# Chunked scans joined into long ones, a modulation product moved from the output projection into the router, and unread products in layer two's router

## The chip, the cores and the metric

The kernel runs on one core of one Trainium2 chip, as a single launch. The metric is device time in microseconds (us), the median of the runs. The profile comes from one further execution that was recorded instruction by instruction. TensorE (PE in the profile), VectorE (DVE), ScalarE (ACT) and GpSimd (POOL) run beside each other; SyncE (SP) only issues transfers, as do GpSimd's queue entries marked DMA.

## The reference, cut to what matters

Two layers over 256 context tokens and 512 latent tokens, 1024 wide. The last layer needs only the latents' output.

```python
for l in range(DEPTH):                                  # DEPTH = 2
    mod   = silu(c)     @ w_ada[l] + b_ada[l]           # six shifts, scales and gates of 1024
    mod_c = silu(c_ctx) @ w_ada[l] + b_ada[l]           # the same for the context
    ...
    u = modulated_rmsnorm(x, ...) @ w_in[l]             # one combined projection
    # mLSTM, 4 heads, chunkwise: for each direction
    bc = jnp.cumsum(to_chunks(log_f), axis=-1)          # running sums that restart at every chunk
    m_t = jnp.maximum(inter, jnp.max(dlog, axis=-1))    # a running maximum of i - b inside the chunk
    h = h * rsqrt(mean(h * h) + EPS) * g_hnorm
    # convolution of width 31 + layernorm, and a 2-D Fourier mix, beside it
    x = x + gt1 * (mix_x @ w_out[l])                    # output projection
    # expert choice: every expert takes its top tokens
    aff = softmax(xn @ w_router); gate, idx = top_k(aff.T, 2 * n // 16)
    hid = silu(xs @ w_gate) * (xs @ w_up)               # 16 experts, xs the chosen rows
    x = x + gt2 * scatter(hid @ w_down * gate)
```

## The kernel before, in words

**Projections.** `w_in` and then `w_out` are read in blocks of 128 output columns. Each block's weights are split into a rounded part (ScalarE copy, L424) and the rest (VectorE subtraction, L425), two buffers deep: `next_w` asks for the split of the next block when a block begins, so that a split has one block's time, about 11 us in layer one, to be ready. The products are L490. `w_out` has eight blocks; VectorE adds each to the residual stream (L1234), ScalarE squares it (L1249).

**Work beside the products.** TensorE's order is the order in which the program issues. A generator that has something to do for TensorE is wrapped in a `Fill`: after each product step it gets credit in microseconds and issues as long as the credit lasts; `run_us(t)` issues about t us of it at once, `drain()` all that is left. On the other engines a scheduler sets the order when the kernel is built, each engine runs its list strictly in that order, and an instruction that waits holds all behind it.

**The chain.** `chain()` is the mLSTM of a layer, issued beside `w_in`. It takes the gates (128 rows: two directions by heads, 768 tokens in 6 chunks of 128), makes the running sums (12 scans of 64x128, L648 and L649) and running maxima (12 more, L655 and L657), state scans over the chunks (L669 to L672), and three exponentials of 128x768 on ScalarE: `WS` (L689), `FL` (L691) and `WI` (L694). Then `to_tokens` transposes the keys head by head (TensorE L626) into two banks that ScalarE copies out (L627). After the heads come the Fourier part (L885 on, copied out at L928), the convolution's layernorm (L950 is its first product; it needs the convolution, 62 VectorE operations at L1027), and the scaling of the heads' outputs (L878) ahead of their transposes.

**Layer two's modulation.** Its `w_ada`, 48 tiles of 0.5 MB, is needed late and is taken during layer one. Round 0 is `ada1()`: 16 loads of 0.5 MB issued by GpSimd (L284) and products on TensorE (L286, eight groups of 16 matmuls in the trace) beside layer one's `w_out`, then a small sum (L295). Rounds 1 and 2 are `ada1_rest()`: 32 loads (L1136) that VectorE multiplies and adds up (L1139 for the first of a run of eight, L1141 for the other seven), and `ada1_sums()` on TensorE (L1150, L1158).

**The router.** Logits are gathered during `w_out` and transposed (L1284); a softmax on VectorE and ScalarE gives the affinities, which TensorE transposes (L1311); VectorE finds the top tokens in rounds (L1318 to L1321) while TensorE transposes all tokens (L1335), copied out by ScalarE (L1336); the indices are transposed (L1357), and GpSimd gathers the rows (L1425, layer one) or TensorE selects them by products with one-hot matrices (L1433, L1448, layer two). The first expert's rows are transposed at L1451 in layer one.

**The experts.** SP loads weights in tiles of 1 MB (L1203) into a ring; `wide()` computes the products (L1505, L1515).

```python
fills.append(ada1f)          # round 0: beside layer one's w_out, at a rate
...
if not last:
    ada1f.run_us(ADA_XTK)    # what is left of it, after L1335
...
if not last:
    ada1f.drain()            # after L1357
```

## Time and profile before

| | us |
|---|---|
| median of three runs (lowest, highest) | 1813.42 (1810.08, 1815.36) |
| the profiled execution's own time | 1820.03 |
| its span in the trace | 1818.1 |
| TensorE busy | 1708.9 (94%) |
| VectorE busy | 655.8 (36%) |
| ScalarE busy | 445.1 (24%) |
| GpSimd busy | 124.2 (7%) |

The span runs from the first recorded instruction to the last; the profiled execution's own time is 1.9 us more. Times of day in the rows below are us from the span's start. [...]

### The profile page before, as it was taken

The numbers are of one execution on the slowest core, as the hardware profiler recorded it, in microseconds if no ns is written. First come the engines' busy times: TensorE is split into PE (matmuls) and PEld (weight loads), VectorE is DVE, ScalarE is ACT, GpSimd is POOL, SyncE is SP. The second block draws the span as 40 slices with busy tenths as digits, with TensorE's granted clock in tenths as the row PEclk, the third lists the DMA queues.
The fourth block names the chain that finished last, engine by engine and source line by source line (L and its number), as shares of the span: only waits on it lengthen the run. The fifth ranks groups of instructions, "written<-read, shape, count | busy, mean of one in ns | idle before, by whom it ended". The sixth has DMA issues, their size and how long they took to land. (4 is left out here: it accounts for less than half of the span.)

```text
span 1818.1 us, 27372 instructions
## 1 busy us (share of the span) xinstructions
PE 1708.9 (94%) x11544; PEld 944.9 (52%) x11544; DVE 655.8 (36%) x1420; ACT 445.1 (24%) x864; POOL 124.2 (7%) x183
## 2 busy tenths in 40 slices
PE   6989998997999999999899989989989999999997
PEld 3678986776333333333233467877644444344434
DVE  4623889754101001000013676965230222112213
ACT  4532453513101101011010553355221000010002
POOL 1011111210101101100100000020000000000000
PEclk8999999998899999999999999999989999999997
DMA  9456335944999999999995112243669999999993
GB/s 384 167 203 209 100 99 184 360 175 163 395 420 401 402 421 403 402 415 408 400 396 214 36 55 79 81 120 132 240 249 420 420 420 420 421 421 420 420 421 156
DMA packets 94523, 529.58 MB, mean 291 GB/s; under 512 B 10176, under 2 KB 13248, under 8 KB 45504
## 3 DMA queue, kind: packets, MB, share of 16 engines
q1 hardware_dynamic: 75776, 459.66, 62.9%
q0 software_dynamic: 18624, 68.17, 11.4%
q8 instruction: 91, 1.49, 0.3%
q14 instruction: 32, 0.26, 0.0%
HBM read 513.10 MB, written 14.68 MB: 290 GB/s over the span
## 5 line engine op out<-in xcount | busy, mean ns | idle before, releaser
L490 PE MATMUL PS<-RA,RB 128*128 128x512 f32 (+1 forms) x2352 | 517.5, 367 | 11.4 <-DVE RB L425 6.1
L490 PEld LDWEIGHTS PS<-RA,RB 128*128 128x128 f32 x2352 | 378.7, 193 | 87.0 <-issue 16.0
L1505 PE MATMUL PS<-A 128*32 128x512 f32 (+1 forms) x2264 | 410.0, 595 | 4.4 <-DMA A<-w_e_up 3.9
L1505 PE MATMUL PS<-WP,A 128*32 128x512 f32 (+1 forms) x2152 | 351.6, 597 | 4.0 <-DMA WP<-w_e_up 4.0
L1505 PEld LDWEIGHTS PS<-A 128*32 128x32 f32 (+1 forms) x2264 | 123.9, 122 | 236.4 <-issue 220.2
L1505 PEld LDWEIGHTS PS<-WP,A 128*32 128x32 f32 (+1 forms) x2152 | 102.0, 117 | 200.6 <-issue 189.4
L1515 PE MATMUL PS<-WP,A 128*32 128x512 f32 x816 | 112.3, 594 | 0.0
L1027 DVE SCALAR_TENSOR_TENSOR A<-A 128x783 f32<-128x783 f32 (+1 forms) x120 | 103.5, 888 | 0.1
L1456 ACT ACTIVATE A<-PS,A 128x128 f32<-128x128 f32 x80 | 35.9, 457 | 250.8 <-DVE A L1458 250.1
L1515 PE MATMUL PS<-A 128*32 128x512 f32 x656 | 95.0, 606 | 0.0
L424 ACT ACTIVATE RB<-A 128x1024 fp32r<-128x1024 f32 x60 | 63.3, 1058 | 128.4 <-PE PS L490 118.6
L1558 ACT ACTIVATE A<-PS 128x512 f32<-128x512 f32 x40 | 22.3, 595 | 294.0 <-PE PS L1557 294.0
L1604 DVE TENSOR_SCALAR A<-PS,A 128x512 f32<-128x512 f32 x6 | 4.5, 751 | 243.9 <-PE PS L1505 243.9
L1578 DVE SCALAR_TENSOR_TENSOR RB<-PS,A,RB 128x512 fp32r<-128x512 f32 x18 | 13.5, 750 | 205.7 <-ACT RB L1577 204.8
L1571 DVE SCALAR_TENSOR_TENSOR A<-PS,A 128x512 f32<-128x512 f32 x80 | 56.4, 746 | 86.2 <-PE PS L1570 85.6
L1458 DVE TENSOR_SCALAR A<-PS,A 128x128 f32<-128x128 f32 x80 | 32.6, 410 | 145.0 <-PE PS L1451 89.5
L425 DVE TENSOR_TENSOR RB<-A,RB 128x1024 fp32r<-128x1024 f32 x60 | 73.2, 1223 | 20.1 <-ACT RB L424 17.6
L1448 PEld LDWEIGHTS PS<-A 128*128 128x128 f32 x512 | 59.5, 196 | 7.2 <-DVE A L1549 4.9
L1448 PE MATMUL PS<-A 128*128 128x128 f32 x512 | 61.2, 281 | 0.4 <-DVE A L1435 0.4
L1549 DVE TENSOR_TENSOR A<-PS,A 128x512 f32<-128x512 f32 x32 | 22.1, 692 | 109.3 <-PE PS L1505 109.3
L1515 PEld LDWEIGHTS PS<-WP,A 128*32 128x32 f32 x816 | 27.9, 110 | 54.6 <-issue 54.6
L1570 PE MATMUL PS<-RB 128*128 128x512 f32 x160 | 46.4, 416 | 5.4 <-ACT A L1456 4.3
(343 smaller groups left out, 1576.5 us busy)
## 6 DMA issues: line engine op xcount, KB each, us to landing
A<-w_e_gate SPq DMA_DIRECT2D x73, 1024.0 KB, 17.3
A<-w_e_down SPq DMA_DIRECT2D x71, 1024.0 KB, 19.8
A<-w_e_up SPq DMA_DIRECT2D x65, 1024.0 KB, 15.8
WP<-w_e_up SPq DMA_DIRECT2D x63, 1024.0 KB, 15.5
WP<-w_e_gate SPq DMA_DIRECT2D x55, 1024.0 KB, 18.3
WP<-w_e_down SPq DMA_DIRECT2D x55, 1024.0 KB, 17.2
A<-w_ada POOLq DMA_DIRECT2D x80, 512.0 KB, 5.8
A<-w_in SPq DMA_DIRECT2D x44, 512.0 KB, 3.6
```

The source lines that it names most:

```text
L424: whi.append(act.activation(h, raw[i], AF.Copy))
L425: wlo.append(dve.tensor_tensor(lo, raw[i], h.bitcast(F32), OP.subtract))
L490: pe.matmul(banks[s][:, :LEN[s]], w[:, k], xin[:, j, k, OFF[s]:OFF[s] + LEN[s]], start=k == k0 and i == 0, stop=k == k1 and i == 2)
L1027: dve.scalar_tensor_tensor(o, i, wcol, o, op0=OP.mult, op1=OP.add)
L1448: pe.matmul(b[:, j], XT[2 + c][:, db * 128:db * 128 + 128], onehots[i][:, c], start=c == 0, stop=c == 3)
L1456: act.activation(dst[:, db], b[:, j], AF.Identity, bias=sh_, scale=sc_)
L1458: dve.tensor_scalar(dst[:, db], b[:, j], sc_, sh_, op0=OP.mult, op1=OP.add)
L1505: pe.matmul(B(o + hf)[c:c + wd, :], lhs(k, e)[:, c % 64:c % 64 + wd], w[e][:, a, hf * 512:hf * 512 + 512], start=k == 0, stop=k == KB - 1, ...
L1515: pe.matmul(B(o + 2)[32 * g:32 * g + 32, :], lhsc(k, e), w[e][:, a, hf * 512:hf * 512 + 512], start=k == 0, stop=k == KB - 1, tile_positio ...
L1558: act.activation(dst, b, AF.Copy)
L1570: pe.matmul(b, YS[:, j, db * 128:db * 128 + 128], PM if pm is None else pm, start=j == 0, stop=j == 1)
L1571: dve.scalar_tensor_tensor(X[LAT][:, db], b, MOD[l][:, LAT, 40 + db:41 + db], X[LAT][:, db], op0=OP.mult, op1=OP.add)
```

## The change

1. The 24 short scans of a layer become four scans of 64x768, two for the sums and two for the maxima. Two vectors of 768 that GpSimd writes (`RS`, ones with a zero at each chunk's start, and `RM`, zeros with -1e30 there) make them restart at each chunk.
2. The exponentials of `WI` and `FL` are tied behind the copies of the first and the second head's transposes, where they stood ahead of all of them.
3. The scaling at L878 (24 of 128x128 in layer one, 16 in layer two) goes from VectorE to ScalarE.
4. Round 0 of layer two's modulation leaves `w_out`. Its 16 loads get buffers of their own (nine and six of the former two rings and one more), are issued by GpSimd when the seventh of the eight blocks is reached in the program, and its products stand in three places of layer one's router: 24 matmuls after L1284, 24 after L1335, 16 after L1357, there with the sums of rounds 1 and 2 (L1150, L1158), which also leave `w_out`.
5. In layer two's router, three products of `ones` by a 512-wide tile are issued after L1284 and five after L1335, into a bank that nobody reads.

```diff
@@ chain()
+                for t, x, y in ((RS, 1.0, 0.0), (RM, 0.0, -1e30)):
+                    pool.memset(t, x)
+                    pool.memset(t[0:64, 0:TT:128], y)
+                    pool.memset(t[64:128, 127:TT:128], y)
...
-                for c in range(6):
-                    x0, x1 = c * 128, c * 128 + 128
-                    dve.tensor_tensor_scan(b_[fw, x0:x1], ones[fw], LF[fw, x0:x1], 0.0, op0=OP.mult, op1=OP.add)
...
+                dve.tensor_tensor_scan(b_[fw], RS[fw], LF[fw], 0.0, op0=OP.mult, op1=OP.add)
+                dve.tensor_tensor_scan(b_[bw][:, ::-1], RS[bw][:, ::-1], LF[bw][:, ::-1], 0.0, op0=OP.mult, op1=OP.add)
...
+                dve.tensor_tensor_scan(M[fw], RM[fw], a_[fw], -1e30, op0=OP.add, op1=OP.max)
...
-                after(act.activation(FL, FL, AF.Exp, scale=-1.0), kev, NOSYNC)
...
-                after(act.activation(WI, WI, AF.Exp), kev, NOSYNC)
                 for h in range(H):
                     yield from to_tokens(kT[:, h], h, KT)
+                    if h == 0:
+                        after(act.activation(WI, WI, AF.Exp), [kev[-1], tok[-1]], NOSYNC)
+                    if h == 1:
+                        after(act.activation(FL, FL, AF.Exp, scale=-1.0), [tok[-1]], NOSYNC)
...
-                            dve.tensor_scalar(hh, hh, SS[:, c0 + c, h:h + 1], None, op0=OP.mult)
+                            act.activation(hh, hh, AF.Copy, scale=SS[:, c0 + c, h:h + 1])
@@ layer two's modulation
+                def ada1_loads():
+                    for i in range(2 * KB):
+                        w0.append(V((areg[6:] + areg[:6] + [w0_r])[i], 4, 256))
+                        pool.dma_start(w0[i], w_ada[1, 0, i // KB, i % KB].rearrange("p (g c) -> p g c", g=4))
                 def ada1():
-                    yield from ada_round(1, 0, Ring(areg[:6]), 5, pool, some=ADS[1])
+                    ps = B(5)
+                    for i, w in enumerate(w0):
+                        k, hf = i % KB, i // KB
+                        for g in range(4):
+                            pe.matmul(ps[32 * g:32 * g + 32, hf * 256:hf * 256 + 256], cs[:, k, :], w[:, g],
+                                      start=k == 0, stop=k == KB - 1, tile_position=(0, 32 * g))
+                        if i % 2:
+                            yield 0.95
...
+                    yield from sums
...
-                fills.append(ada1f)
@@ w_out
                 if db == KB - 2 and not last:
                     ada1v.drain()
-                    fills.append(Fill(ada1_sums(), 0.6))
+                    ada1_loads()
@@ router
+            if last:
+                keep_up(3)
+            if not last:
+                ada1f.run_us(ADA_XTK[0])
...
+            if last:
+                keep_up(5)
...
-                ada1f.run_us(ADA_XTK)
+                ada1f.run_us(ADA_XTK[1])
...
+            def keep_up(n):
+                for _ in range(n):
+                    pe.matmul(B(7), ones, iot, start=True, stop=True)
```

How the change moves instructions, at two places. The first is layer one's chain. On VectorE, before, from the last of the running sums to the first of the running maxima (scans are listed as SCALAR_TENSOR_TENSOR; L425 is a weight split):

```order
L648 SCALAR_TENSOR_TENSOR A<-A 64x128
L649 SCALAR_TENSOR_TENSOR A<-A 64x128
L668 COPY A<-A 64x6
L651 TENSOR_TENSOR A<-A 128x768
L668 COPY A<-A 64x6
L425 TENSOR_TENSOR RB<-A,RB 128x1024
L655 SCALAR_TENSOR_TENSOR A<-A 64x128
```

and after (L653 and L654 are the long sums, L657 and L658 the long maxima, L670 the first state scan, L424 the weight split that was L425):

```order
L654 SCALAR_TENSOR_TENSOR A<-A 64x768
L669 COPY A<-A 64x6
L655 TENSOR_TENSOR A<-A 128x768
L666 MEMSET A 128x6
L669 COPY A<-A 64x6
L657 SCALAR_TENSOR_TENSOR A<-A 64x768
L658 SCALAR_TENSOR_TENSOR A<-A 64x768
L668 COPY A<-A 64x6
L676 MEMSET A 64x1
L668 COPY A<-A 64x6
L670 SCALAR_TENSOR_TENSOR A<-A 64x5
L424 TENSOR_TENSOR RB<-A,RB 128x1024
```

The split, which stood between sums and maxima, stands behind both. On ScalarE at the same place, before, from the table load ahead of the exponentials to the first copies of the keys' transposes:

```order
L684 ACT_TABLE_LOAD
L684 ACTIVATE A<-A 128x6
L689 ACTIVATE A<-A 128x768
L691 ACTIVATE A<-A 128x768
L694 ACTIVATE A<-A 128x768
L627 ACTIVATE A<-PS 128x2x128
L627 ACTIVATE A<-PS 128x4x128
```

and after (L690 is the exponential of `WS`, L626 the copies that were L627, L697 and L699 the other two exponentials):

```order
L685 ACT_TABLE_LOAD
L685 ACTIVATE A<-A 128x6
L690 ACTIVATE A<-A 128x768
L626 ACTIVATE A<-PS 128x2x128
L626 ACTIVATE A<-PS 128x4x128
L697 ACTIVATE A<-A 128x768
L626 ACTIVATE A<-PS 128x2x128
L626 ACTIVATE A<-PS 128x4x128
L699 ACTIVATE A<-A 128x768
```

Two exponentials have gone behind the first two and the first four copies. The second place is layer one's router. On TensorE, before, from the last logits to the first expert's rows:

```order
L1211 MATMUL PS<-A 32x512 x4
L1215 MATMUL PS<-A 32x512 x4
L1284 MATMUL PS<-A,WP_3273 128x17 x6
L1311 MATMUL PS<-A,WP_3273 96x128 x2
L1335 MATMUL PS<-A 128x128 x48
L1357 MATMUL PS<-A,WP_3274 128x96 x2
L1451 MATMUL PS<-A,WP_3274 128x128 x8
```

and after (L1317 is the former L1284, L1348 the former L1311, L1372 the former L1335, L1396 the former L1357; L1138 and L1148 are round 0, L1182 and L1190 the sums that were L1150 and L1158). A row of the list counts a float32 product once, which the trace shows as two instructions:

```order
L1317 MATMUL PS<-A,WP_3157 128x17 x6
L1138 MATMUL PS<-A 32x256 x24
L1348 MATMUL PS<-A,WP_3157 96x128 x2
L1372 MATMUL PS<-A 128x128 x48
L1138 MATMUL PS<-A 32x256 x24
L1396 MATMUL PS<-A,WP_3158 128x96 x2
L1138 MATMUL PS<-A 32x256 x16
L1182 MATMUL PS<-A 32x256 x16
L1148 MATMUL PS<-A 128x8 x4
L1190 MATMUL PS<-A 128x8 x8
L1490 MATMUL PS<-A,WP_3158 128x128 x8
```

All of the moved products stand in these three gaps. On GpSimd, before, the last loads of the modulation ahead of the router (L284 round 0, L1136 rounds 1 and 2):

```order
L1136 DMA A<-w_ada 128x1024
L284 DMA A<-w_ada 128x1024 x2
L1136 DMA A<-w_ada 128x1024 x7
L1278 MEMSET WP_3273 128x192
L1399 MEMSET A 128x16
```

and after (L1130 the loads of round 0, L1168 those of rounds 1 and 2):

```order
L1130 DMA A<-w_ada 128x1024
L1168 DMA A<-w_ada 128x1024 x8
L1130 DMA A<-w_ada 128x1024 x2
L1168 DMA A<-w_ada 128x1024
L1130 DMA A<-w_ada 128x1024 x4
L1168 DMA A<-w_ada 128x1024 x21
L1130 DMA A<-w_ada 128x1024
L1168 DMA A<-w_ada 128x1024
L1130 DMA A<-w_ada 128x1024 x8
```

Seven of round 0's sixteen loads are issued early, and nine, which go into the buffers of rounds 1 and 2, at the end, behind the last of those.

## Rows read from the trace of the kernel before

**Rows 1.** The page, part 1: busy us, share of the span, instructions of TensorE

```profile
PE 1708.9 (94%) x11544; PEld 944.9 (52%) x11544; DVE 655.8 (36%) x1420; ACT 445.1 (24%) x864; POOL 124.2 (7%) x183
```

**Rows 2.** Timeline, 74 to 97 us: start, us, engine, line, operation, idle before

```profile
76.01 0.42 DVE L648 TENSOR_TENSOR_SCAN A<-A 64x128 f32<-64x128 f32 x1
...
82.48 1.23 DVE L425 TENSOR_TENSOR RB<-A,RB 128x1024 fp32r<-128x1024 f32 x1
...
86.70 1.19 ACT L985 ACTIVATE A<-PS 128x512 f32<-128x512 f32 x1 [8.55 <-PE PS L490]
...
93.07 0.95 DVE L693 TENSOR_TENSOR A<-A 128x768 f32<-128x768 f32 x1
...
94.67 0.83 ACT L694 ACTIVATE A<-A 128x768 f32<-128x768 f32 x1
95.41 0.85 ACT L627 ACTIVATE A<-PS 128x256 f32<-128x256 f32 x2
...
95.82 0.69 PE L626 MATMUL PS<-A 128*128 128x128 f32 x2 [4.47 <-ACT A L627]
```

**Rows 3.** Busy by stretch, with TensorE's clock and the DMA share, around 98 us

```profile
96.00:102.00 6.00, 6.00 (x23) 5.23 (x24) 0.00 (x0) 1.56 (x4) 0.34 (x1) 0.53 1.00 390
```

**Rows 4.** Group of a short scan on VectorE: total busy us, mean ns

```profile
L669 DVE TENSOR_TENSOR_SCAN A<-A 64x5 f32<-64x5 f32 x1 | 0.2, 160 | 0.0
```

**Rows 5.** Timeline at the convolution's end, VectorE and TensorE

```profile
305.89 2.64 DVE L878 TENSOR_SCALAR A<-A 128x128 f32<-128x128 f32 x13
...
306.04 2.08 PE L950 MATMUL PS<-A 128*128 128x512 f32 x2 [5.55 <-DVE A L1027]
```

**Rows 6.** Timeline on ScalarE, Fourier part before the convolution's end

```profile
288.58 0.60 ACT L928 ACTIVATE A<-PS 128x512 f32<-128x512 f32 x1 [5.54 <-PE PS L926]
```

**Rows 7.** Groups on TensorE in layer one's output projection, 337 to 430 us

```profile
L286 PE MATMUL PS<-A 128*32 128x256 f32 x128 | 9.3, 413 | 0.0
...
L1150 PE MATMUL PS<-A 128*32 128x256 f32 x32 | 1.9, 382 | 0.0
L1158 PE MATMUL PS<-A 128*128 128x8 f32 x16 | 1.8, 251 | 0.0
...
L295 PE MATMUL PS<-A 128*128 128x8 f32 x8 | 1.0, 245 | 0.0
```

**Rows 8.** Groups on VectorE in the same stretch

```profile
L1141 DVE SCALAR_TENSOR_TENSOR A<-A 128x1024 f32<-128x1024 f32 x19 | 24.3, 1283 | 5.4 <-DMA A<-w_ada 5.2
```

**Rows 9.** Busy over the whole of the same projection

```profile
337.00:430.00 93.00, 92.87 (x643) 72.71 (x641) 49.06 (x65) 18.98 (x34) 13.99 (x27) 0.96 0.51 191
```

**Rows 10.** Timeline on TensorE in layer one's router

```profile
438.29 0.63 PE L1311 MATMUL PS<-A,WP 128*96 128x128 f32 x2 [3.30 <-DVE WP L1306]
...
449.87 0.58 PE L1357 MATMUL PS<-A,WP 96*128 96x96 f32 x2 [2.99 <-ACT WP L1354]
457.54 1.97 PE L1451 MATMUL PS<-A,WP 128*128 128x128 f32 x8 [7.09 <-DMA WP<-xrow,A]
```

**Rows 11.** Timeline of SP, the queue of the expert weights

```profile
460.22 3.01 SPq L1203 DMA_DIRECT2D WP<-w_e_gate  x2
```

**Rows 12.** Timeline on TensorE in layer two's chain

```profile
1088.05 7.64 PE L490 MATMUL PS<-RA,RB 128*128 128x512 f32 x25 [4.61 <-DVE RB L425]
...
1100.37 0.44 PE L626 MATMUL PS<-A 128*128 128x128 f32 x2 [3.31 <-ACT A L627]
```

**Rows 13.** Busy by stretch behind these two waits

```profile
1088.00:1092.00 4.00, 3.95 (x10) 3.18 (x11) 2.00 (x2) 0.00 (x0) 0.10 (x1) 0.57 0.64 165
1101.00:1106.00 5.00, 5.00 (x22) 3.99 (x21) 0.00 (x0) 1.59 (x4) 0.72 (x1) 0.66 0.40 131
```

**Rows 14.** Timeline on TensorE in layer two's router

```profile
1333.71 5.51 PE L1448 MATMUL PS<-A 128*128 128x128 f32 x32 [0.45 <-DVE A L1435]
...
1343.31 3.84 PE L1448 MATMUL PS<-A 128*128 128x128 f32 x32
```

**Rows 15.** Busy by stretch in layer one's experts

```profile
560.00:660.00 100.00, 100.00 (x920) 32.10 (x916) 8.19 (x15) 11.30 (x21) 10.04 (x8) 1.00 1.02 408
```

More of the change, by code (lines that the diff above doesn't have):

```diff
@@ L48 @@
 ADS = 2, 2
-ADA1_RATE, AREG, ADA_XTK = 0.3, 15, 1.2
+AREG, ADA_XTK = 15, (2.8, 2.8)
 NACC = 6
@@ L52 @@
 VLAG = 0.0, 2.5
-ADA1_LATE = 2.0
 WORDER = [[KB0 + i for i in range(4)] + p + [QB + i for i in range(4)] + [FB, FB + 1] + [OB + i for i in range(4)]
@@ L614, in body @@
             keep = {}
-            kev = []
+            kev, tok = [], []
             convq = []
@@ L626, in to_tokens @@
                         pe.transpose(p[:, c], src[:, (c0 + c) * 128:(c0 + c + 1) * 128], ident)
-                    act.activation(dst[:, c0:c0 + n, h, 0:128], p[:, 0:n], AF.Copy)
+                    tok[:] = [act.activation(dst[:, c0:c0 + n, h, 0:128], p[:, 0:n], AF.Copy)]
                     yield 0.22 * n
@@ L635, in chain @@
             def chain():
+                rs_r, RS = new(TT)
+                rm_r, RM = new(TT)
+                for t, x, y in ((RS, 1.0, 0.0), (RM, 0.0, -1e30)):
+                    pool.memset(t, x)
+                    pool.memset(t[0:64, 0:TT:128], y)
+                    pool.memset(t[64:128, 127:TT:128], y)
                 lf_r, LF = new(TT)
@@ L645, in chain @@
                 fw, bw = slice(0, 64), slice(64, 128)
-                for c in range(6):
-                    x0, x1 = c * 128, c * 128 + 128
-                    dve.tensor_tensor_scan(b_[fw, x0:x1], ones[fw], LF[fw, x0:x1], 0.0, op0=OP.mult, op1=OP.add)
-                    dve.tensor_tensor_scan(b_[bw, x0:x1][:, ::-1], ones[bw], LF[bw, x0:x1][:, ::-1], 0.0,
-                                           op0=OP.mult, op1=OP.add)
+                dve.tensor_tensor_scan(b_[fw], RS[fw], LF[fw], 0.0, op0=OP.mult, op1=OP.add)
+                dve.tensor_tensor_scan(b_[bw][:, ::-1], RS[bw][:, ::-1], LF[bw][:, ::-1], 0.0, op0=OP.mult, op1=OP.add)
                 dve.tensor_tensor(a_, G, b_, OP.subtract)
                 M = LF
-                for c in range(6):
-                    x0, x1 = c * 128, c * 128 + 128
-                    dve.tensor_tensor_scan(M[fw, x0:x1], a_[fw, x0:x1], a_[fw, x0:x1], -1e30,
-                                           op0=OP.max, op1=OP.max)
-                    dve.tensor_tensor_scan(M[bw, x0:x1][:, ::-1], a_[bw, x0:x1][:, ::-1], a_[bw, x0:x1][:, ::-1],
-                                           -1e30, op0=OP.max, op1=OP.max)
+                dve.tensor_tensor_scan(M[fw], RM[fw], a_[fw], -1e30, op0=OP.add, op1=OP.max)
+                dve.tensor_tensor_scan(M[bw][:, ::-1], RM[bw][:, ::-1], a_[bw][:, ::-1], -1e30, op0=OP.add, op1=OP.max)
+                mem.free([rs_r, rm_r])
                 sm_r, sm = new(4, 6)
@@ L1120, in body @@
                 areg = [mem.alloc(1024) for _ in range(AREG)]
-                def ada1():
-                    yield from ada_round(1, 0, Ring(areg[:6]), 5, pool, some=ADS[1])
+                w0_r, w0 = mem.alloc(1024), []
+                def ada1_loads():
+                    for i in range(2 * KB):
+                        w0.append(V((areg[6:] + areg[:6] + [w0_r])[i], 4, 256))
+                        pool.dma_start(w0[i], w_ada[1, 0, i // KB, i % KB].rearrange("p (g c) -> p g c", g=4))
+                def ada1():
+                    ps = B(5)
[6 more added lines that the diff above has]
+                            yield 0.95
+                    rows_r, rows = new(512)
+                    act.activation(rows, ps, AF.Copy)
+                    sums = ada1_sums()
+                    yield next(sums)
+                    p2 = ps[:, 0:32].rearrange("p (b v g) -> p b v g", b=4, v=2)
+                    for b in range(4):
+                        pe.matmul(p2[:, b], rows[:, b * 128:(b + 1) * 128], selg[:, 0], start=True, stop=True)
+                    for v in range(2):
+                        dve.tensor_tensor(MOD[1][:, v, 0:16].rearrange("p (g b) -> p g b", g=4),
+                                          p2[:, :, v, :].rearrange("p b g -> p g b"),
+                                          bada(1, 0, 16).rearrange("p (g b) -> p g b", g=4), OP.add)
+                    mem.free(rows_r)
                     ada_scale(1, A1[1], 1, P_G1)
+                    yield 0.9
+                    yield from sums
                 acc_r, ACC = new(2, 2, 1024)
@@ L1165, in ada1_sums @@
                     yield 1.5
-                ada1f = Fill(ada1(), ADA1_RATE)
-                ada1f.credit = -ADA1_LATE
-                fills.append(ada1f)
+                ada1f = Fill(ada1(), 1.0)
                 ada1v = Fill(ada1_rest(), ADA1V_RATE)
@@ L1254, in body @@
                 fills[-1].drain()
-                mem.free([areg[6:], acc_r])
             fills.clear()
@@ L1360, in body @@
                 ada1f.drain()
-                mem.free(areg[:6])
+                mem.free([areg, acc_r, w0_r])
             GXu = GX.bitcast(mybir.dt.uint32)
```

## The prediction

> **What bounds the kernel now.** I began with the page: TensorE is busy for 1708.9 of 1818.1 us [rows 1], so time can only come from its work or from the 109 us in which it stands, and a stretch at half clock counts as work. So I read where TensorE stands, what ended each wait, and what its clock did behind it. Four places touch the change. In layer one's chain TensorE stands 4.47 us for ScalarE's copy L627, which runs only after three exponentials, and these only after 18 us of VectorE work from the first scan (76.01) to L693's end (94.02) [rows 2]; behind that stop, 6 us go by at a mean clock of 0.53 [rows 3]. In layer two's chain it stands 4.61 us for a weight split and 3.31 us for the same copy [rows 12], again with a low clock behind [rows 13]. At the convolution's end it stands 5.55 us [rows 5]. In the output projection of layer one it never stands (92.87 of 93 us busy), while the modulation's products run there [rows 7, 9]. Then layer one's router: waits of 3.30, 2.99 and 7.09 us [rows 10], after which SP goes on with the expert weights [rows 11] into a stage in which TensorE and the transfers are both full [rows 15]. Nothing in that stage can take up a later or an earlier start, so what is gained ahead of it moves its end too.
>
> **Long scans.** A scan over 5 elements takes 0.16 us [rows 4], over 128 elements 0.42 [rows 2]: 0.26 us for 123 elements, 2.1 ns each. For 768 that gives 0.42 + 640 x 0.0021 = 1.77 us. The bounds are 0.95, the ordinary 128x768 operation L693, and 6 x 0.42 = 2.5 [rows 2]; I take 1.77, because both scan rows lie on that line. A layer then spends 4 x 1.77 = 7.1 us where it spent 24 x 0.43 = 10.3: 3.2 us less. [...] GpSimd's memsets for the restart vectors stand early in a queue whose engine is busy 124 us in all [rows 1], so I cost them at nothing; were they late, the first long scan would wait by as much.
>
> **Layer one's chain.** The order listing puts the weight split behind all four scans. From 76.01 it is 7.1 us of scans, 1.3 of small operations (the last short sum ends near 76.0 + 12 x 0.43 = 81.2, the split begins at 82.48) and about 0.6 more, so the split starts near 85.0 and ends near 86.2. The block that needs it starts when the one ahead is done, which ScalarE's L985 marks at 86.70 [rows 2]. So no wait, with some 0.4 us to spare. L693 ends at 94.02 - 3.2 = 90.8, L687 ahead of it near 89.9. Behind it there is now one exponential, not three: 0.83 us, held a little by the table load, done near 91.3, and the first copy (half of 0.85) near 91.7 [rows 2]. TensorE stood from 95.82 - 4.47 = 91.35, so 4.1 us of 4.47 go. Without the stop the clock should not fall: 6 x (1 - 0.53) = 2.8 us [rows 3]. The other two exponentials (0.74 apart) now stand between the copies and may hold TensorE for part of that; of 6.9 us I take **6.5** (bounds 3.5 and 7.5).
>
> **Convolution's end.** VectorE drops 24 scalings of 0.20 us (2.64 / 13); 13 come after the convolution, 11 ahead of it [rows 5], 2.2 us. One modulation step (at most a 1.28 us L1141 [rows 8], probably the shorter L1139) moves ahead of its end. I take **1.3** (0 to 2.2). Their place on ScalarE: 14 of them ahead of the last L928 of the latents, which waits 5.54 us for TensorE [rows 6]. Priced at the nearest row, half of L627's pair, 0.43 [rows 2], they take 6.0 and would make it 0.5 late, which VectorE, running its additions in between, would feel. [...]
>
> **Layer one's output projection.** 128 + 32 + 16 + 8 matmuls go: 9.3 + 1.9 + 1.8 + 1.0 = **14.0** us [rows 7]. As TensorE is busy throughout, they come off in full if nothing else becomes late. VectorE is busy 49 us there [rows 9], with 19 of the 32 vector steps of rounds 1 and 2 as L1141 [rows 8] and a few as L1139; by the order listing all but one lie there now, at most 11 or 12 more of 1.28, some 64 us in a stretch of 79. Bounds: 12, if a third of that slack is lost to transfers that come late (5.4 us of idle now [rows 8]), and 16 with the weight loads' gaps.
>
> **Layer one's router.** The 64 moved matmuls are eight groups' worth, 24 of them 3/8 of about 8.6 us, 3.2 us: that is the 3.30 us ahead of L1311 and a little over the 2.99 ahead of L1357. The remaining 16 and the sums are 2.1 + 1.9 + 0.5 + 1.8, some 6.5 us, in the 7.09 us wait for the gather [rows 7, 10]. So they cost at most 0.2, and TensorE stays awake: L1451, 1.97 us at half clock, twice, would be nearer 1.0. What of this is on the path of the transfers (460.22 [rows 11]) I can't read; I take **1.0** (from 2 lost to 3 won).
>
> **Layer two's chain.** The scans bring 3.2 us; the split that ended the 4.61 us wait goes behind L693 in the new order, 0.9 back: 2.3 won. The second wait loses two exponentials, 1.5 of 3.31 [rows 12, 2]. Half clock behind them: 4 x 0.43 and 5 x 0.34, 1.7 each [rows 13]. Of 7.2 I take **6.8**; if stops of some 2 us still bring the clock down, 3.8; if the scan costs 2.5 us, less.
>
> **Unread products.** The second batch of selections, L1448, takes 3.84 us at full clock, the first 5.51 [rows 14]; a warm TensorE brings **1.7** (0 to 2).
>
> **Sum.** 6.5 + 1.3 + 14.0 + 1.0 + 6.8 + 1.7 = 31.3 us. The profiled execution took 1820.0, so 1788.7; it lay 6.6 above the median of the runs shown, so the forecast median is **1782**.
>
> **Rivals.** *Loads come last (chance 0.17).* Nine of round 0's loads, the nine used first, stand in GpSimd's queue behind the last vector load and wait for VectorE's last reads. In the new order the vectors begin behind the projection's first split, which I put at 6 us into the stretch, 343; the 64 us of VectorE work, less some 5 to 10 that belongs to the last blocks, end them near 397 to 402; nine tiles of 0.5 MB at 390 GB/s [rows 3] take 12 us: they land near 410 to 415. TensorE wants the first behind L1284, at 438.3 - 3.3 - 14.0 = 421 [rows 10]. With 6 to 10 us to spare this is not comfortable; if VectorE waits for transfers as it does now, the spare is gone. TensorE's queue is in order, so each us late holds L1311, the top-k, the gather and the expert weights: 8 late gives 1790. This is the rival on the other side too: slower than before once the tiles are over 31 us late, landing after 452 (0.03 of the 0.17). Against it: transfers are busy only 0.51 of that stretch [rows 9].
>
> *A long scan costs 2.5 us (0.10).* Then the split in layer one ends near 89.2, 2.6 us after its block could start, and the first wait in layer two stays whole: 2.2 and 4.0 less gain, 1788.
>
> *The clock doesn't hold (0.08).* Short stops and narrow products don't keep it up: 2.8, 3.4 and 1.7 us come back, and the 6.5 us drained behind L1357 take 13 for a wait of 7.09: 1791 at worst. For it: it is low at L1451 now although L1335 ran not long before.
>
> *The exponentials only move (0.05).* With `WI` and `FL` between the copies, TensorE waits at each later head for what it no longer waits at the first: 3 us and 1.5 less, 1787.
>
> **How the numbers follow.** The rest, 0.60, is the forecast, with a range of its own of 1775 to 1789 from the bounds of its terms. The range for 8 in 10 takes in the rivals' prices: 1773 to 1795. A change below 0.3% (5.4 us) can't be told from none here. Faster by more than that in every case but late loads of over 26 us: 0.94; within it 0.03, slower 0.03.
>
> **What would show it.** Right: L626 in layer one's chain without a stop of over 1 us, clock 1.00 to 102; L1451 at about 1 us; no L286 or L1150 in the projection, about 79 us long; first L1448 of layer two below 4.2. Wrong: TensorE waiting for DMA of w_ada ahead of L1311, or for L425 inside `w_out`, or a long scan well off 1.8.

## The result and the profile after

| | before | after |
|---|---|---|
| median, us (lowest, highest; 4 runs each) | 1814.39 (1810.08, 1816.47) | 1786.05 (1785.18, 1790.9) |
| the profiled execution's own time | 1820.03 | 1785.22 |
| its span in the trace | 1818.1 | 1783.4 |
| mean granted clock of TensorE over the span (1.00 is full speed) | 0.969 | 0.983 |

The ratio of the times is 0.9861, with a 95% interval of 0.9839 to 0.9882: 25.2 us of 1814.4 are gone, between 21.4 and 29.2. The forecast was 1782 in a range of 1773 to 1795. The page after, part 1, beside [rows 1]:

```profile
PE 1695.7 (95%) x11560; PEld 935.3 (52%) x11560; DVE 642.8 (36%) x1340; ACT 457.0 (26%) x904; POOL 127.0 (7%) x195
```

TensorE has lost 13.2 us of busy time, the span 34.7; the other 21.5 are waits.

**Layer one's chain.** Timeline after, VectorE, ScalarE and TensorE, beside [rows 2]:

```profile
71.78 1.75 DVE L653 TENSOR_TENSOR_SCAN A<-A 64x768 f32<-64x768 f32 x1
...
80.77 1.20 DVE L424 TENSOR_TENSOR RB<-A,RB 128x1024 fp32r<-128x1024 f32 x1
...
82.37 1.22 ACT L988 ACTIVATE A<-PS 128x512 f32<-128x512 f32 x1 [8.55 <-PE PS L489]
...
85.65 0.95 DVE L693 TENSOR_TENSOR A<-A 128x768 f32<-128x768 f32 x1
...
86.35 0.83 ACT L690 ACTIVATE A<-A 128x768 f32<-128x768 f32 x1
87.08 0.85 ACT L626 ACTIVATE A<-PS 128x256 f32<-128x256 f32 x2
...
87.50 0.44 PE L625 MATMUL PS<-A 128*128 128x128 f32 x2 [0.49 <-ACT A L626]
```

A long scan takes 1.75 us. The split behind the scans (80.77) ends at 81.97, 0.4 us ahead of ScalarE's L988, which marks the next block. The first copy comes behind one exponential, and TensorE stands 0.49 us where it stood 4.47. The windows behind it, the columns as in [rows 3]:

```profile
88.00:94.00 6.00, 6.00 (x48) 4.53 (x47) 0.00 (x0) 3.26 (x6) 1.10 (x3) 1.00 1.01 362
```

The clock is 1.00 where it was 0.53.

**Output projection and router of layer one.** Timeline after, GpSimd, VectorE and TensorE, beside [rows 10, 11]:

```profile
384.97 0.53 POOL L1130 DMA_DIRECT2D A<-w_ada  x1 [0.79 <-DVE A L1173]
...
408.04 2.80 PE L1138 MATMUL PS<-A 128*32 128x256 f32 x48
411.43 0.40 PE L1348 MATMUL PS<-A,WP 128*96 128x128 f32 x2 [0.58 <-DVE WP L1343]
...
422.78 0.39 PE L1396 MATMUL PS<-A,WP 96*128 96x96 f32 x2 [0.84 <-ACT WP L1393]
...
425.85 1.04 POOL L1464 DMA_INDIRECT WP<-xrow,A  x1 [19.65 <-DVE A L1430]
...
427.60 2.21 PE L1190 MATMUL PS<-A 128*128 128x8 f32 x16
...
431.75 0.17 DVE L1192 TENSOR_TENSOR A<-PS,A 128x16 f32<-128x16 f32 x1 [1.82 <-remote]
...
433.24 0.17 DVE L1192 TENSOR_TENSOR A<-PS,A 128x16 f32<-128x16 f32 x1 [1.24 <-remote]
...
433.47 1.97 PE L1490 MATMUL PS<-A,WP 128*128 128x128 f32 x8 [3.66 <-DVE A L1192]
```

The last of round 0's loads is issued at 384.97, and loads of this line land 5.5 us after their issue in the median of that stretch; TensorE begins with their products at 408.04, without a wait. So the loads have 17 us to spare. The moved products fill the waits of 3.30 and 2.99 us down to 0.58 and 0.84. The third wait, 7.09 for the gather, is now 3.66 for something else: the first expert's transposes (L1490) write the two banks from which VectorE still adds the sums (L1192). It does so late: TensorE's sums end at 429.8, and between them and the additions VectorE sits idle for 1.82 and 1.24 us that the profile gives to no engine of this core ("remote"). L1490 still takes 1.97 us, as in [rows 10], and the clock over it is 0.50 in both (433.4 to 435.5 us; 457.5 to 459.6 before).

**Layer two.** Timeline after, TensorE, beside [rows 12, 14]:

```profile
1057.29 7.65 PE L489 MATMUL PS<-RA,RB 128*128 128x512 f32 x25 [2.26 <-DVE RB L424]
...
1068.15 0.44 PE L625 MATMUL PS<-A 128*128 128x128 f32 x2 [1.85 <-ACT A L626]
...
1298.16 0.61 PE L1396 MATMUL PS<-A 64*128 64x64 f32 x2 [1.84 <-ACT A L1389]
...
1301.62 6.22 PE L1487 MATMUL PS<-A 128*128 128x128 f32 x32 [0.44 <-DVE A L1474]
...
1311.93 3.84 PE L1487 MATMUL PS<-A 128*128 128x128 f32 x32
```

The two waits of the chain are 2.26 and 1.85 us (4.61 and 3.31 before). In the router the first batch of selections took 6.22 us, not less than the 5.51 of before.

**Where the time went, stage by stage.** Each number is the time from one instruction's start to the next one's in the trace. The columns end with: the chain's first operation; the convolution's first VectorE operation; the first block of `w_out` added to the residual stream; the last logits; the first expert's transposes; the chain's first operation in layer two; the first block of its `w_out`; its first selections; its experts' first products; the last product. The rows named "again" and "third" are further executions, which belong to the experiments below.

```
                start  chain 1   conv   w_out  router 1  experts 1  chain 2  proj. 2  router 2  experts 2
before          73.96   123.61  148.94  84.84    26.19    610.11    199.57    66.49     6.01     454.73
before again    71.50   123.14  149.63  81.99    26.32    608.45    202.55    66.73     6.01     454.76
after           69.62   116.96  147.74  70.16    28.99    605.79    195.95    66.41     6.73     454.72
after again     69.86   116.92  146.11  71.74    28.80    608.79    192.42    66.11     6.00     454.74
after third     68.84   116.97  147.68  70.16    26.68    609.91    192.53    66.11     6.00     454.86
scans           71.31   118.40  147.12  83.83    26.04    609.66    196.50    67.08     5.49     454.55
exponentials    72.99   120.90  149.52  84.37    26.22    608.72    196.64    66.74     5.52     454.69
chain           72.76   116.94  146.56  83.89    25.83    609.56    194.75    67.09     6.36     454.74
modulation      70.34   122.95  148.58  67.87    26.72    609.31    199.81    66.55     5.73     454.63
unread          74.28   123.71  149.68  82.60    26.13    608.67    199.05    66.49     6.07     454.76
scaling         71.69   116.95  146.73  70.17    28.84    607.58    193.00    66.10     5.81     454.72
sum banks       69.68   116.97  147.70  70.18    27.30    609.32    195.17    66.41     6.32     454.56
longer          70.16   116.95  147.77  70.17    28.85    607.96    192.63    66.38     4.45     454.57
both            69.25   116.97  147.57  70.17    26.98    610.09    193.56    66.32     4.44     454.70
```

The columns chain 1 and w_out show the two large gains. Most of the others differ as much between two executions of one kernel as between kernels.

### The profile page after: what moved, and what is told of

Same layout as the page of the kernel before. It is cut to its first block, busy times and chain, and to the rows that moved or that the text cites. A ratio compares the mean times of both kernels' runs of the same rounds, so it can differ in the third digit from the quotient of the medians.

```text
span 1783.4 us, 27391 instructions
## 1 busy us (share of the span) xinstructions
PE 1695.7 (95%) x11560; PEld 935.3 (52%) x11560; DVE 642.8 (36%) x1340; ACT 457.0 (26%) x904; POOL 127.0 (7%) x195
## 5 line engine op out<-in xcount | busy, mean ns | idle before, releaser
L489 PE MATMUL PS<-RA,RB 128*128 128x512 f32 (+1 forms) x2352 | 507.4, 363 | 9.0 <-DVE RB L424 3.8
L489 PEld LDWEIGHTS PS<-RA,RB 128*128 128x128 f32 x2352 | 373.3, 190 | 80.2 <-issue 12.0
L424 DVE TENSOR_TENSOR RB<-A,RB 128x1024 fp32r<-128x1024 f32 x60 | 73.3, 1226 | 24.3 <-ACT RB L423 21.9
```

The source lines that it names most:

```text
L424: wlo.append(dve.tensor_tensor(lo, raw[i], h.bitcast(F32), OP.subtract))
L489: pe.matmul(banks[s][:, :LEN[s]], w[:, k], xin[:, j, k, OFF[s]:OFF[s] + LEN[s]], start=k == k0 and i == 0, stop=k == k1 and i == 2)
```

## The experiments

### One part at a time

**The scans alone** (part 1 on the kernel before).

```diff
-                for c in range(6):
...
+                dve.tensor_tensor_scan(b_[fw], RS[fw], LF[fw], 0.0, op0=OP.mult, op1=OP.add)
...
+                dve.tensor_tensor_scan(M[fw], RM[fw], a_[fw], -1e30, op0=OP.add, op1=OP.max)
```

> The kernel before with the long scans alone (exponentials, modulation, scaling and router as before). If the changed kernel's trace is read rightly, four scans of 1.76 us take the place of 24 at a pitch of 0.43: VectorE is 3.3 us earlier behind the chain's scans. Layer one: TensorE's stop at the first head's copies, 4.47 us before, shrinks to 1.2 to 1.5 us and the clock behind it stays at 1.00: 6 us less. Layer two: the stop for the weight split goes from 4.61 to 2.3 us, the stop for the copy stays at 3.3 with the low clock behind it: 2.3 us less. In all 8 us less than before (0.45%). Rival, that the scans and the moved exponentials only work together: layer one's stop stays above 3 us and the clock still falls, 5 us less or under.

Measured: 1802.83 us beside 1813.89, ratio 0.9944 (0.9923 to 0.9965). Layer one's chain is 5.2 us shorter (118.40 against 123.61): TensorE's stop at the first copies is 1.95 us, a little more than expected, and the clock behind it stays at 1.00 (92 to 108 us), so the theory held and the rival fell. Layer two's chain is 3.1 us shorter (196.50 against 199.57).

**The exponentials alone** (part 2).

```diff
-                after(act.activation(WI, WI, AF.Exp), kev, NOSYNC)
...
                     yield from to_tokens(kT[:, h], h, KT)
+                    if h == 0:
+                        after(act.activation(WI, WI, AF.Exp), [kev[-1], tok[-1]], NOSYNC)
```

> The kernel before with two of the three exponentials behind the heads' copies, and nothing else. Each of the two stops for the first copy loses two exponentials of 0.74: 4.47 becomes 3.0 in layer one and 3.31 becomes 1.85 in layer two. Behind the 3.0 us stop I expect the low clock to remain (1.5 us less in layer one), behind the 1.85 us stop I expect 1.00 as in the changed kernel (3.2 us less in layer two): 4.7 us less in all (0.26%). Rival: the exponentials only move, and TensorE stops at the second and third head for what it saved: no less than 1 us gained.

Measured: 1806.45 us, ratio 0.9966 (0.9949 to 0.9983). Layer one's chain is 2.7 us shorter: the stop is 3.02 us, and around it the clock falls (0.62 from 92 to 96 us), as the theory had it. Layer two's chain is 2.9 us shorter.

**Both together** (parts 1 and 2 by the two diffs above, and nothing else).

> The kernel before with parts 1 and 2 alone (long scans; two exponentials behind the copies). The single parts gave 5.2 and 2.7 us in layer one's chain and 5.5 and 3.2 in layer two's by their profiles. Theory: both shorten the same wait and the same stretch at half clock behind it, so they don't add up: 6.6 in layer one and 5 to 7 in layer two as in the changed kernel, 12 to 13.5 us, a ratio of 0.9926 to 0.9934. Rival: they add up, 16.6 us, a ratio of 0.9908. Against both, gains in layer two's chain may be given back up to its output projection, as 1 to 2 us were in the changed kernel; then 0.994.

Measured: 1799.23 us beside 1813.16, ratio 0.9921 (0.991 to 0.9933). Layer one's chain is 6.7 us shorter (116.94), as in the changed kernel, and not 5.2 + 2.7 = 7.9: the parts overlap. The interval just leaves out the 0.9908 expected of a sum, but not 0.9910, the product of the two ratios measured alone; the overlap rests on the stage.

**The modulation alone** (part 4).

```diff
-                fills.append(ada1f)
...
-                    fills.append(Fill(ada1_sums(), 0.6))
+                    ada1_loads()
...
+                ada1f.run_us(ADA_XTK[0])
```

> The kernel before with the modulation's move alone. If it acts as in the changed kernel: the output projection about 15.4 us shorter, layer one's router 2.8 us longer because the first expert's transposes wait for the modulation's last sums on VectorE, about 12.6 us less in all (0.7%). Rival, that the 2.8 us came of the shifted start of that router or of chance: L1451 in this kernel starts when the gather lands, some 4.4 us behind its issue, and the gain is 14 to 16 us.

Measured: 1796.22 us, ratio 0.9916 (0.9894 to 0.9938), 15.2 us by the ratio (the medians lie 17.7 apart). The output projection takes 67.87 us where the two executions of before took 84.84 and 81.99. The rival described it: the first expert's transposes start with the gather's rows, though 5.4 us behind its issue (431.11 to 436.46). This ratio times that of parts 1 and 2 together is 0.9838, just below the interval of the whole change (0.9839 to 0.9882): the parts don't add up in full.

**The unread products alone** (part 5).

```diff
+            if last:
+                keep_up(3)
...
+            if last:
+                keep_up(5)
```

> The kernel before with the unread products alone. If the changed kernel shows the rule: the clock stays at 1.00 until L1357 and falls then, because TensorE has some 1.8 and 1.6 us without work on both sides of it, so the first batch of selections runs at half clock as a whole, 6.2 us instead of 5.5: 0 to 0.7 us slower, which the times can't tell from no change. Rival, my forecast: the batch at full clock, 3.84 us, 1.7 us less.

Measured: 1812.54 us, ratio 0.9998 (0.9987 to 1.0009). Nothing. The first batch of selections takes 5.57 us (5.51 before), their stage 6.07 (6.01 before).

### Parts changed in the changed kernel

**The scaling back on VectorE** (the changed kernel without part 3).

```diff
-                            act.activation(hh, hh, AF.Copy, scale=SS[:, c0 + c, h:h + 1])
+                            dve.tensor_scalar(hh, hh, SS[:, c0 + c, h:h + 1], None, op0=OP.mult)
```

> The changed kernel with the scaling of the heads' outputs back on VectorE. By my sum for the convolution's end it is 11 x 0.20 us of VectorE work that returns ahead of it, less what waits hide: TensorE's stop there grows from 5.1 to about 6.5 us, 1.3 us slower. Rival: VectorE's waits for ScalarE's Fourier copies hide it, and the stop stays within 0.5 us of 5.1.

Measured: 1787.11 us beside 1811.14, ratio 0.9875 (0.9859 to 0.9892), against 0.9862 (0.9845 to 0.9878) of the changed kernel run beside it: not told apart. TensorE's stop at the convolution's end is 5.56 us, within 0.5 of 5.1 as the rival had it. With the scaling on VectorE the convolution's part (conv) is 146.73 us long, within the 146.11 to 147.74 of the three executions of the changed kernel.

**The sums in other banks.** The sums of rounds 1 and 2 go to the banks 0 and 1, which the first expert's transposes don't use.

```diff
-                        p2 = B(6 + r)[:, 0:32].rearrange("p (b v g) -> p b v g", b=4, v=2)
+                        p2 = B(r)[:, 0:32].rearrange("p (b v g) -> p b v g", b=4, v=2)
```

> The changed kernel with the last sums of rounds 1 and 2 written to banks 0 and 1 instead of 6 and 7, which the first expert's transposes use. If those transposes are late because VectorE still reads their bank, they now start when the gather lands, 1.5 us earlier at least: 1.5 to 3 us less. Rival: the wait was not for the bank but for VectorE's place in its queue or for the gather; then nothing changes beyond 0.5 us.

Measured: 1784.54 us, ratio 0.9853 (0.9837 to 0.987). The time can't be told from the changed kernel's; the profile can. Timeline on TensorE, and VectorE's additions:

```profile
431.58 0.17 DVE L1192 TENSOR_TENSOR A<-PS,A 128x16 f32<-128x16 f32 x1 [1.64 <-remote]
...
431.83 1.97 PE L1490 MATMUL PS<-A,WP 128*128 128x128 f32 x8 [2.14 <-DMA WP<-xrow,A]
```

VectorE is as late as before, but TensorE no longer waits for it: it starts with the gather's rows, 1.7 us earlier in the router's stage (27.30 against 28.99). So TensorE's wait was for the bank.

**More unread products.** Seven instead of five behind L1372, and two behind the copy ahead of the one-hot products.

```diff
             if last:
-                keep_up(5)
+                keep_up(7)
...
+            if last:
+                keep_up(2)
```

> The changed kernel with seven instead of five unread products behind the token transposes and two more behind the transposed indices, so that TensorE has no stop of over 0.7 us from the logits to the selections. If the clock fell for lack of work in the 1.8 and 1.6 us stops, it now stays at 1.00 and the first batch of selections takes 3.84 us as the second does, 2.4 us less than in the changed kernel and some 0.2 us given back by the index transposes: 2 us less in all, 0.1%. Rival: the clock falls all the same, since selections by narrow products follow, and nothing is gained.

Measured: 1785.27 us, ratio 0.9867 (0.9846 to 0.9888). The first batch of selections, in the timeline on TensorE:

```profile
1300.87 3.94 PE L1489 MATMUL PS<-A 128*128 128x128 f32 x32 [0.65 <-DVE A L1476]
```

3.94 us, near the 3.84 of the changed kernel's second batch, whose clock is 1.00 (1311.9 to 1315.8 us), and the stage takes 4.45 instead of 6.0. The idea of part 5 works once no thin stretch is left behind the products, but 1.6 us are too few for the times to show. Which of the two additions is needed was not tried.

**Both corrections together** (the diffs of the two kernels above).

> The change as it is, with both small corrections together: the sums of rounds 1 and 2 go into the banks 0 and 1 in place of 6 and 7, and layer two's router has two more unread products behind L1372 and two behind the copy ahead of its gather. If the two act at different places and each is kept to the end, the profile shows the first expert's transposes 1.7 us earlier and layer two's first batch of selections 1.6 us shorter, and the time lies 2 to 3 us under the change's, 1782 to 1784 beside a kernel before of 1811 to 1814 (ratio 0.984 to 0.985). Rival: the earlier transposes are swallowed by the experts' stage, where TensorE and the transfers are both full and the weights were issued as before; then only 1.6 us are left and the time can't be told from the change's, 1784 to 1786.

Measured: 1783.48 us (1782.41 to 1787.99) beside 1813.16, ratio 0.9842 (0.9827 to 0.9856). The profile shows both stages shorter: router 1 takes 26.98 us, router 2 4.44. But what router 1 gains is gone by the end of the experts, as the rival had it: router 1 and experts 1 together take 637.1 us, and 634.8, 637.6 and 636.6 in the three executions of the changed kernel. This is the lowest median of all kernels here, but its interval overlaps that of the changed kernel (0.9845 to 0.9878), so it is not shown to be faster.

### How much of a profile is chance

**The changed kernel again**, unaltered.

> The changed kernel once more, unaltered. Two stretches of its trace may be chance: the start, 4.3 us shorter than before up to the first scan, where none of the edits lies, and the 3.2 us by which the first expert's transposes in layer one's router start late behind a wait of VectorE that the trace puts to no engine. If the start is chance it comes out anywhere from 0 to 4 us shorter than before. If the late transposes are due to the move, VectorE's two last sums of the modulation again wait over 1 us each and TensorE stands over 3 us for them; if they are chance, TensorE starts when the gather lands, some 5 us behind its issue, and the median over more runs lies below the 1786 of the first four by 1 to 2 us.

Measured: 1785.59 us, ratio 0.9862 (0.9845 to 0.9878).

**Each kernel profiled once more**, unaltered.

> The kernel before, profiled once more. The question is the start: up to the chain's first operation (L642) the profiled execution of before took 73.96 us, the changed kernel's 69.62, with no costed edit there; behind waits for w_ada the clock was 0.68 and 0.64 from 35 to 45 us in the one and 1.00 in the other. Theory: which executions lose the clock there is chance, and that is also why the profiled execution of before lay 6.6 us above its median; then a new execution of the same kernel lies anywhere from 71 to 74 us, and its total time goes with it, 1811 to 1819. Rival: the kernel before loses the clock there every time, and the change gains 3 to 4 us at the start by something I have not costed; then it is 73.5 to 74.5 again.

Measured: 1816.67 us. The start took 71.50 us, not 73.96. The windows of the first execution of before and then of the new one show what differed:

```profile
35.00:40.00 5.00, 3.13 (x21) 1.65 (x22) 4.12 (x10) 4.16 (x8) 0.00 (x0) 0.68 1.02 419
40.00:45.00 5.00, 5.00 (x21) 4.29 (x19) 0.22 (x1) 0.00 (x0) 0.00 (x0) 0.64 1.03 410
360.00:370.00 10.00, 10.00 (x55) 7.76 (x55) 7.81 (x9) 0.47 (x1) 1.58 (x3) 0.66 0.62 221
```

```profile
35.00:40.00 5.00, 2.89 (x26) 1.81 (x27) 4.12 (x10) 4.61 (x9) 0.00 (x0) 1.00 1.03 420
40.00:45.00 5.00, 4.50 (x33) 3.41 (x32) 1.11 (x6) 0.46 (x2) 0.00 (x0) 1.00 1.03 410
360.00:370.00 10.00, 10.00 (x75) 7.33 (x74) 8.83 (x8) 0.00 (x0) 3.88 (x8) 1.00 0.78 263
```

The same kernel lost its clock at the start and in the output projection in one execution and not in the other. The start is 2.46 us shorter and w_out 2.85 (the table's rows). The whole execution is only 3.4 us shorter, since layer two's chain took 3.0 more: chance goes both ways, and the 6.6 us by which the first profiled execution lay above the median can't be put down to two stages.

> The changed kernel, profiled a third time, beside the kernel before of the same call. Two executions had the chain's first operation at 69.62 and 69.86 us with a clock of 1.00 from 35 to 45. By chance alone the third may as well lie at 72 to 74; by the rival it is below 70.5 again. The second question is layer two's start and chain: in the first execution the clock held at layer two's start and fell behind the 2.26 us stop of the chain, in the second it was the other way about, with the sum within 1 us. By chance the third is one of the two, and the sum again within 1 us.

Measured: 1785.17 us. The start took 68.84 us, below 70.5 again. All eight profiles with part 4 lie between 68.8 and 71.7 (mean 69.9), the six without it between 71.3 and 74.3 (mean 72.8). So not all of the start is chance in the profiles; what part 4 does there was not found. Up to the chain, TensorE, VectorE and ScalarE run the same instructions in the same order in before and in the modulation's kernel. It may also be smaller in the other executions: where there are several, the profiled one lies 0.4 to 5.6 us above its kernel's median without part 4, most where the start was longest (73.96 and 74.28), and between 2.5 below and 1.5 above with it. Layer two went as in the second execution: experts 1 and chain 2 together take 801.7, 801.2 and 802.4 us in the three. The router's additions were on time in this execution, which is new; timeline on VectorE and TensorE:

```profile
427.89 0.18 DVE L1192 TENSOR_TENSOR A<-PS,A 128x16 f32<-128x16 f32 x1 [0.20 <-PE PS L1190]
...
430.33 1.94 PE L1490 MATMUL PS<-A,WP 128*128 128x128 f32 x8 [1.65 <-DMA WP<-xrow,A]
```

No "remote" wait, and TensorE waits for the gather. In the modulation's own kernel it was so too. So VectorE's lateness comes in most executions (six of the seven of the changed kernel and its variants) but not in all, and the bank turns it into a wait of TensorE.

## Why the prediction was right, and where it was not

**Right: the long scans and layer one's chain.** 1.77 us was forecast for a scan from two short rows [rows 2, 4]; it takes 1.75 us. The split had 0.4 us to spare, as forecast. The chain gained 6.65 us (123.61 to 116.96) for a term of 6.5. Of the 6.9, TensorE's later heads took little back: no copy behind the exponentials held it for over half a us in that stretch (its waits for L626 from 87 to 190 us are 0.5 us in all).

**Right: layer one's output projection.** 14.0 us of matmuls came off. Where the clock held, 81.99 (before again) against 67.87 (modulation), the stage is 14.1 shorter, though one of the eight groups of L286 lies ahead of its first mark. The changed kernel's own 70.16 is 2.3 longer than 67.87; there the clock was 0.83 from 346 to 356 us (0.69 and 0.83 in its other two executions), in the modulation's kernel 1.00, and 10 us at 0.83 cost 1.7 by estimate (10 x 0.17). The windows of the changed kernel, then of the modulation's:

```profile
346.00:356.00 10.00, 10.00 (x53) 8.78 (x53) 9.12 (x10) 1.05 (x2) 2.22 (x5) 0.83 0.93 331
```

```profile
346.00:356.00 10.00, 10.00 (x70) 9.17 (x70) 6.11 (x9) 1.99 (x3) 2.12 (x4) 1.00 0.82 283
```

TensorE is busy throughout, but what it does ahead of the fall is 32 narrow products for the router, of 16 columns each. Timeline on TensorE, the first execution of before (where the clock falls at 361 us), then the changed kernel:

```profile
358.45 4.48 PE L1230 MATMUL PS<-A 128*128 128x16 f32 x32
```

```profile
343.89 3.64 PE L1264 MATMUL PS<-A 128*128 128x16 f32 x32
```

In eleven of the fourteen profiles the clock falls to 0.50 there, beginning between 2.0 us before the end of these products and 0.4 us after it, and nowhere else in the stage. In before again, modulation and unread it holds at 1.00, with the same products; what decides it is open. By the means of all profiles, falls included, w_out went from 83.6 us (six without the move) to 70.4 (seven of the changed kernel and its variants), 13.2 us.

**Refuted: "Loads come last".** The rival gave the loads 6 to 10 us to spare; they have 17, since VectorE works almost without a wait. Its group in the projection after, beside [rows 8]:

```profile
L1173 DVE SCALAR_TENSOR_TENSOR A<-A 128x1024 f32<-128x1024 f32 x28 | 35.3, 1281 | 0.4
```

28 instead of 19 of the long steps, with 0.4 us of idle ahead of them instead of 5.4.

**Right: layer two's chain.** 6.8 us was forecast. The first execution shows 199.57 to 195.95, only 3.6, with the clock down behind the 2.26 us stop (0.57 from 1057 to 1061 us; 7.65 us for 25 products), the case that the prediction put at 3.8. That was this execution's: in the second the same stop is there and the products take 6.11 us. Over all executions with parts 1 and 2 and the modulation the stage takes 192.4 to 196.0 (mean 193.6 of seven), and 199.1 to 202.6 over the four of kernels without parts 1 and 2 (mean 200.2): 6.6. The timeline of the second execution of the changed kernel:

```profile
1060.25 6.11 PE L489 MATMUL PS<-RA,RB 128*128 128x512 f32 x25 [2.26 <-DVE RB L424]
1069.57 0.44 PE L625 MATMUL PS<-A 128*128 128x128 f32 x2 [1.85 <-ACT A L626]
```

**Wrong: the convolution's end, 1.3 us.** The step "VectorE drops 24 scalings" counted VectorE's time as the path. The wait is 5.13 us instead of 5.55 [rows 5], and 5.56 without part 3: 0.4 us, which neither the times nor the stages show. The stage conv did become shorter, 149.3 to 147.2 in the means of two and three executions, but the kernels with the scans alone (147.12) and with parts 1 and 2 (146.56) have that too, and the exponentials alone don't (149.52): it belongs to the scans, and no step forecast it there. ScalarE's scalings were cheaper than the row they were priced at: 14 in 4.20 us, 0.30 each, where 0.43 was the price; ScalarE stood 1.44 us between them and the copy (L931, the former L928) that 6.0 us would have made 0.5 late. Timeline on ScalarE and TensorE:

```profile
272.28 4.20 ACT L881 ACTIVATE A<-A 128x128 f32<-128x128 f32 x14
277.93 0.60 ACT L931 ACTIVATE A<-PS 128x512 f32<-128x512 f32 x1 [1.44 <-issue]
...
294.96 2.07 PE L953 MATMUL PS<-A 128*128 128x512 f32 x2 [5.13 <-DVE A L1030]
```

That the gain went into VectorE's waits for the Fourier copies, which TensorE paces, is likely and was not tried.

**Wrong: layer one's router, 1.0 us won.** The stage lost 2.8 in the first execution and 0.5 in the third. The failed step is "So they cost at most 0.2, and TensorE stays awake". The sums do fit into the gather's time on TensorE, but I followed only TensorE's order and not who reads the banks afterwards. Their late reading is worth 1.7 us of the stage by the kernel with other banks, and 2.3 between the first and the third execution. TensorE's clock rose (0.93 in the mean from the last logits to L1490, 0.71 before) but did not hold to the end: TensorE still stood 1.65 us ahead of the transposes in the third execution, and L1490 took 1.94 us there. And the gather's rows came later after their issue: 4.4 us before (issued at 453.13 by the timeline on GpSimd, used at 457.54 [rows 10]), 5.3 in the third execution (425.00 to 430.33).

**Wrong: "Nothing in that stage can take up a later or an earlier start".** The experts' stage of layer one did. In the four profiles with the move in which the transposes are late for the bank (after, after again, scaling, longer), router 1 takes 28.9 us in the mean and experts 1 607.5; in the four others (after third, modulation, sum banks, both) 26.9 and 609.7. The sums are 636.4 and 636.6: by the end of the experts the wait for the bank costs nothing that these sums show. Without the move the sum is 635.3 in the mean of six. So the move costs about 1.2 us there where 1.0 was to be won; why is open.

**Wrong: the unread products, 1.7 us.** They cut TensorE's waits ahead of L1348 and L1396 from 2.97 and 5.05 us to 0.30 and 1.84, and the clock was 1.00 up to 1298 us, but it falls from L1396 on, among the small operations ahead of the selections. The failed step is "a warm TensorE brings 1.7": TensorE didn't stay warm up to the selections. The windows after:

```profile
1298.00:1302.00 4.00, 1.72 (x6) 1.15 (x6) 3.07 (x15) 0.11 (x1) 0.00 (x0) 0.73 0.01 2
1302.00:1306.00 4.00, 4.00 (x20) 4.00 (x20) 0.73 (x3) 0.00 (x0) 0.00 (x0) 0.50 0.00 0
```

TensorE is busy for 1.72 of 4 us in the first of these stretches, at a clock of 0.73, and then goes at 0.50. The kernel with products there too gains 1.6 of the 1.7.

**The sum.** By the profiles' stages 6.65 us came from chain 1, 13.2 from w_out and 6.6 from chain 2; the router and the experts behind it took about 1.2 of that. The scans' 2 in conv and the start's 2.9, which no step had, come on top: 30 us. The two medians lie 28.3 apart, and the interval of the ratio ends at 29.2, with 25.2 as its middle. That the sum of 31.3 came this close is partly luck: the router was mis-sized by 2.2, the unread products by 1.7, the convolution's end by 1.3 and w_out by 0.8, against gains of 2 to 5 that were not seen; the start's part of these may show in the profiled executions alone. 1813.42 less 31.3 is 1782, so the step from the profile to the median did no harm. Between the two profiled executions 34.8 us went, more than the sum; that of before lay 3.4 us above the next execution of the same kernel.

Two small sums of the prediction are off. The drained products and sums in the router, some 6.5 us, add up to 6.3 by the terms given, and to 6.8 with L295 at the 1.0 of its row [rows 7]; either fits into 7.09. And the price of the rival *The clock doesn't hold*, 1791 at worst, leaves out the 5.9 us by which its 13 us exceed the wait of 7.09; with them it is 1796. The forecast stands on neither.

## What to carry to other kernels

When work is moved into another engine's wait, list the buffers it takes until their last reader is done, not only the time it fills: here the sums fitted, and their banks became the wait (3.66 us). Follow a gain or a loss to the end of the next long stage before counting it: here that stage took the wait up (636.4 us with it, 636.6 without, by its end). Here, products that nobody reads brought a faster first batch (3.94 us against 6.22) only when they also covered the thin stretch between the shortened wait and the work they were to speed up. Profile the kernel before twice ahead of pricing a change of 1 to 2%: stages of before differed by up to 3.0 us between its two executions, two of them where the clock differed.

## What the runs showed of the hardware that I had not expected

The granted clock fell in stretches in which TensorE did not wait: 0.66 from 360 to 370 us of before, with 10.00 of 10 us busy, and 1.00 in the next execution of the same kernel. In w_out the fall always came at the 32 products of 16 columns, in eleven profiles of fourteen. Behind a stop of 2.26 us the clock fell (0.57 from 1057 to 1061 us) in one execution of the changed kernel; it held in two others (2.26 and 2.24 us). In layer two, where the changed kernel's first execution held the clock at the beginning (1.00 from 1005 to 1015 us), the second had 0.70, and the clock didn't fall at the later stop (6.11 us for the 25 products behind it, 7.65 in the first).

VectorE's two additions in the router waited 1.2 to 1.8 us after all that the trace shows them waiting for had ended, in most executions, and not in all. What held them is open. So is why the gather's rows took about 1 us longer to land behind the moved products, and what the modulation's move changes in the first 70 us.
